# A hybrid encoder layer: four x tiles normed before the first projection block, the first pair's attention bias on ScalarE's queue, and three score blocks set into a projection

## The chip, the cores and the metric

The kernel runs on one core of a Trainium2 chip. The metric is the device time of one execution in microseconds (us); of several executions the median is given. PE is TensorE (its matmuls; PEld its weight loads), DVE is VectorE, ACT is ScalarE, POOL is GpSimd, SP is SyncE, which does no arithmetic here and issues most transfers (DMAs).

## The reference

One layer over a sequence of 1024 rows with 1024 columns, in float32:

```
h   = rmsnorm(x, norm_mix_w) * (1 + scale_m(c)) + shift_m(c)
P   = h @ w_in                     # z, xbc, dt, q, k, v in one projection
y_s = mamba2_ssd(z, xbc, dt)       # 8 heads of 64
q.. = chunks of 64 rows; each attends to its own chunk and 8 before it, 8 heads of 64
s   = q @ k^T / 8 + rel_bias[head][clipped distance]   # invalid keys: minimum
y_a = softmax(s) @ v
x   = x + gate_m(c) * (concat[y_s, y_a] @ w_out)
h   = rmsnorm(x) * (1 + scale_f(c)) + shift_f(c)
g,v = split(causal_dwconv3(h @ w_up));  x = x + gate_f(c) * ((silu(g) * v) @ w_down)
out = rmsnorm(x)
```

scale, shift and gate are columns of `c @ w_ada`.

## The kernel before

The float32 products are made of rounded parts: a matrix is split into a high part (`hH`, `wsh`, `wh`) and the rest (`hL`, `wsl`, `wl`), and a product is three matmuls (`mm3`: high by high, low by high, high by low). Sequence rows come in 8 tiles of 128 (`xts[0..7]`; the traces call them `qk`, since they share that store), and the 1024 columns in 8 slices `kt`. A half `hh` is four row tiles.

**The opening.** For each `kt` the kernel loads two 512 KB pieces of `w_ada` (`adat`), multiplies each with the row of c and sums it on DVE (`mod_col`, one reduction of 128x1024 each), which gives the column's scale and shift (`amix`, `bmix`); loads the piece of `w_first` (q and k of the first pair and v; `raws`), rounds it on ACT (`wsh`) and takes the rest on DVE (`wsl`). The x tiles are normed row by row: `x_square` (ACT, or DVE as a reduction), `x_rstd` (add EPS on DVE, power -0.5 on POOL), `x_scale` (ACT or DVE). `h_block(hh, kt)` transposes four normed tiles on PE (`tp`), and ACT makes `hH` and `hf` of them with `amix` and `bmix`, DVE `hL`. Then `first_qk` (accumulators `acc`) and `first_v` (`vps`) multiply. For `kt` = 0 this is done in two halves of two tiles: tiles 2 and 3 are loaded after the first weights and normed after the first half's `hH`. `kt` 6 and 7 of `acc` come as a tail, after the v products. Tiles 4 to 7 are loaded and normed amid the later `kt`; their loads wait for a DVE copy (`XL`), their ACT and DVE work for a block (`XS`, `XM`). Before the first block PE runs 8 and then 12 matmuls on the identity (`warm_up`, `WARM`).

**The attention.** A pair `p` is two heads; its 8 blocks `i` of 128 queries attend to up to 640 keys. `attn_scores` does for each block and head: two matmul groups into a `s` tile (`scores`; two such tiles in all, one for each head), a DVE reduction that adds the bias and takes the row's extreme (L529), exp on ACT (L532), a reciprocal on DVE (L534), the scaling on POOL (L535). `attn_pv` transposes the scaled rows on PE (`tp`, L561 and L564), splits them (`pt`, ACT and DVE) and multiplies with v (`pv`). Blocks 0 to 2 of pair 0 take the bias from a small tile that is loaded early (`rows`); from block 3 on it is the tile `bias`, 128x640, one for each head, loaded on SP's queue, and two corners of it are set to -1e30 by POOL (the masks, L591 and L592). `gemm_part(2, 0)` is the projection of a later pair's q: 8 `kt` of three matmuls for each half, in one accumulator `acc`. Between the first half's matmuls and the second's it needs that accumulator copied out by DVE (`ev`, L236).

**What sets the order.** A scheduler places each engine's instructions in one row by its own model of times. `tc.issue_after(x)` holds an instruction behind another one in that order; `InOrder` (`V`, `A`, `T` while `.on`) chains the instructions of an engine in the order of the code, and those have line L61 in the profile, whatever they do. SP's queue issues in its row's order and stops at the first transfer whose buffer or source is not free.

Of the kernel before, what the change touches and what calls it, by code (L numbers as in the profile page):

```python
# [10 lines left out]
F32 = mybir.dt.float32  # L11
# [5 lines left out]
P = 128  # L17
# [12 lines left out]
PRST = 4  # L30
GP, GPL = {0: (0,1), 2: (2,)}, ()
# [3 lines left out]
WARM = (8, 12)  # L35
# [32 lines left out]
def tile_block(ctx: ExitStack, tc: tile.TileContext, x, ccol, pk, w_ada, w_first, w_ft, w_z,  # L68
# [58 lines left out]
    G.memset(mhalf, -0.5)  # L127

# [74 lines left out]
    def mod_shift(dst, sh, kt, n=1):  # L203
        V.tensor_tensor(dst[:, kt:kt + n], modc[:, sh + kt:sh + kt + n],
                        pkt[:, B_ADA + sh + kt:B_ADA + sh + kt + n], ALU.add)
# [55 lines left out]
    def scores(p, i):  # L261
        d = qk[p]
        j0 = max(0, i - 4)
        n = (i - j0 + 1) * P
        off = (j0 - (i - 4)) * P
        parts = [(0, n)] if n <= 512 else [(0, 320), (320, 320)]
        st = [s_tile(), s_tile()]
        for h in range(2):
            for pi, (a, w) in enumerate(parts):
                for ti, kn in enumerate(("kh", "kl")):  # L270
                    T.matmul(st[h][:, 512 * pi:512 * pi + w], d["q"][h][:, i * P:(i + 1) * P],
                             d[kn][h][:, j0 * P + a:j0 * P + a + w], start=ti == 0, stop=ti == 1)
        return st, n, off, parts


# [36 lines left out]
    def x_square(st, eng):  # L312
        ms = stat()
        junk = s0.tile([P, D], F32, tag="junk", name="junk")
        if eng is A:
            i = norm_to(xts[st], junk, ms)
        else:
            i = V.tensor_tensor_reduce(out=junk, in0=xts[st], in1=xts[st], scale=1.0 / D, scalar=0.0,
                                       op0=ALU.mult, op1=ALU.add, accum_out=ms)
        return ms  # L320

    def x_rstd(ms):
        r = stat()
        V.tensor_scalar(ms, ms, EPS, None, op0=ALU.add)
        G.tensor_tensor(r, ms, mhalf[:, 0:1], ALU.pow)
        return r
# [15 lines left out]
    for st in range(2):  # L342
        x_load(st)
# [21 lines left out]
    r0 = x_rstd(ms0)  # L365
    r1 = x_rstd(x_square(1, V))
    x_scale(0, r0, A)
    x_scale(1, r1, A)
# [27 lines left out]
    for hh in range(2):  # L396
# [13 lines left out]
        for kt in range(KT):  # L410
            if hh == 0:
                mod_col(SC_M + kt, wu.tile([P, 1024], F32, tag="wh", name="adat"))
                mod_col(SH_M + kt, adw[:, kt % 2, :])
                V.scalar_tensor_tensor(amix[:, kt:kt + 1], modc[:, SC_M + kt:SC_M + kt + 1],
                                       pkt[:, NMIX + kt:NMIX + kt + 1], am1[:, kt:kt + 1],
                                       op0=ALU.mult, op1=ALU.add)
                mod_shift(bmix, SH_M, kt)
                t = raw_tile(768)
                nc.sync.dma_start(t, w_first[kt])
                split(wsh[:, kt, :], ws_lo(kt), t, A, V)  # L420
                if kt == 0:
                    for st in (2, 3):
                        x_load(st)
                    for b in range(2):
                        if b:
                            with tc.issue_after(hb[0].ins):
                                r = [x_rstd(x_square(st, A)) for st in (2, 3)]
                            x_scale(2, r[0], V)
                            x_scale(3, r[1], V)
                        hb = h_block(0, 0, (2 * b, 2 * b + 1))  # L430
                        T.on = False
                        for n in range(4):
                            first_qk(accs[n], n, 0, (0,), slice(2 * b, 2 * b + 2))
                        first_v(vps, 0, (0,), (b,))
                        V.on = A.on = T.on = False
                    continue
                for st in range(4, NT):
                    if XL[st - 4] == kt:
                        V.tensor_copy(xts[st][:, 0:1], amix[:, kt:kt + 1])
                        x_load(st)  # L440
            if hh == 0 or kt > 1:
                hb = i, last_lo = h_block(hh, kt)
            if hh == 0:
# [71 lines left out]
    def attn_scores(p, i, bt):  # L515
        st, n, off, parts = s00 if p + i == 0 else scores(p, i)
        res = []
        for h in range(2):
# [16 lines left out]
            G.tensor_scalar(pv_, pv_, rr, 1.0, op0=ALU.mult, op1=ALU.mult)  # L535
# [46 lines left out]
    last_v, early = [], {}  # L582
    mtq, todo = [], [m + kt for m in (G_M, SC_F, SH_F, G_F) for kt in range(KT)]

    def attention(p, extra=()):
        extra = dict(extra)
        bt = []
        for h in range(2):
            t = bp.tile([P, 640], F32, tag="bias", name="bias")
            nc.sync.dma_start(t, bias[2 * p + h])  # L590
            G.memset(t[0:64, 576:640], -1e30)  # L591
# [15 lines left out]
    def gemm_ft(wh, wl, outs):  # L607
        for hh in range(2):
            for kt in range(KT):
                w = slice(kt * P, (kt + 1) * P)  # L610
                mm3(c4(outs[hh]), wh[:, w], wl[:, w], *ht(hh, kt), kt == 0, kt == KT - 1)

    def gemm_part(p, which):
# [8 lines left out]
        gemm_ft(wh, wl, outs)  # L622
# [1065 lines left out]
```

## Time and profile before

| | |
|---|---|
| median of 3 runs | 1205.41 us (1205.05 to 1207.55) |
| profiled execution: its own time | 1205.95 us |
| profiled execution: span | 1204.2 us |
| granted TensorE clock, mean | 0.986 of full |
| busy: PE, DVE, ACT, POOL | 1168.7, 909.1, 587.5, 156.5 us |
| DMA | 160.24 MB, mean 133 GB/s |

The span runs from the first to the last instruction; 1.75 us of the execution's own time lie outside it. Of the span PE is idle for about 35.5 us in all. A row of a timeline gives the start in us, the duration, the engine, the line, the operation, output <- inputs by the program's names, and in brackets the idle time before it and what ended it. Matmul records overlap: a row's duration has the matmul's latency in it, and the distance between two starts is the pace. A row of the windows gives, behind the stretch, its length and the busy time (and instructions) of PE, PEld, DVE, ACT and POOL, the granted clock, the busy share of the DMA engines and what they moved in GB/s.

### The profile page before, as it was taken

Reading aid. Unit: us, or ns where it says so; the run is one execution under the profiler, and the core shown is the slowest. Engines: PE = TensorE matmul, PEld = TensorE weight load, DVE = VectorE, ACT = ScalarE, POOL = GpSimd, SP = SyncE. Lnnn points to the kernel's source line nnn. Section 1 sums busy time; section 2 is a strip of 40 time slices with the busy share of each in tenths; the row PEclk is TensorE's granted clock in tenths of the full one; section 3 lists DMA queues with packets and bytes.
Section 4 is the critical chain, followed back from the end, with each engine's and each line's share of the span. In section 5 each row is a group of like instructions: output and inputs, shape, how many; then the busy total and the mean of one; then the engine's idle time right before and its main releaser. Section 6 shows DMA issues by size and latency. Waiting matters only on the chain.

```text
span 1204.2 us, 15722 instructions
## 1 busy us (share of the span) xinstructions
PE 1168.7 (97%) x5823; PEld 980.8 (81%) x5823; DVE 909.1 (75%) x1364; ACT 587.5 (49%) x968; POOL 156.5 (13%) x177
## 2 busy tenths in 40 slices
PE   8998999899999899999999999999999999999996
PEld 6777888788889888888788888888888888888885
DVE  7645565775596888658999988898889879766986
ACT  6534564674243757577534443344333445433454
POOL 1002342530000344200000000000000000000522
PEclk8998999999999989999999999999999999999998
DMA  9635434301486322140232323322233378733443
GB/s 357 244 84 136 110 108 116 108 1 36 153 273 222 124 66 93 53 164 30 79 139 98 102 92 105 131 81 98 94 121 114 110 250 299 258 114 122 158 132 149
DMA packets 61293, 160.24 MB, mean 133 GB/s; under 512 B 6608, under 2 KB 7072, under 8 KB 59808
## 3 DMA queue, kind: packets, MB, share of 16 engines
q1 hardware_dynamic: 54160, 134.85, 34.2%
q10 hardware_dynamic: 7056, 24.38, 5.1%
q8 instruction: 46, 0.75, 0.3%
q14 instruction: 31, 0.25, 0.1%
HBM read 121.15 MB, written 28.61 MB: 124 GB/s over the span
## 4 chain that ended last, share of the span: by engine, by line
PE 85%; DVE 8%; issue 3%; DMA 2%; ACT 1%; SPq 1%; POOL 0%; POOLq 0%; DVEq 0%; ACTq 0%
PE wops L827 6%; PE dn L81 5%; PE dn L79 5%; PE dn L80 5%; PE uY L79 5%; PE uY L81 5%; PE uY L80 5%; PE uX L81 3%; PE uX L79 3%; PE uZ L80 3%; PE uZ L79 3%; PE uX L80 3%; PE uZ L81 3%; PE s L79 3%; PE s L80 3%
## 5 line engine op out<-in xcount | busy, mean ns | idle before, releaser
L80 PE MATMUL dn<-w 128*128 128x512 f32 x296 | 108.1, 392 | 0.0
L79 PE MATMUL dn<-w 128*128 128x512 f32 x296 | 108.1, 391 | 0.0
L81 PE MATMUL dn<-w 128*128 128x512 f32 x296 | 100.2, 391 | 0.2 <-DVE w L89 0.2
L79 PE MATMUL uY<-tH,w 128*128 128x512 f32 x248 | 97.2, 392 | 0.0
L80 PE MATMUL uY<-tL,w 128*128 128x512 f32 x248 | 97.0, 391 | 0.0
L81 PE MATMUL uY<-tH,w 128*128 128x512 f32 x248 | 96.9, 391 | 0.0
L1549 POOL TENSOR_TENSOR ya<-ya,xs 128x512 f32<-128x512 f32 x4 | 17.2, 4330 | 557.6 <-ACT xs L1545 557.6
L88 ACT ACTIVATE w<-ya 128x1024 fp32r<-128x1024 f32 (+1 forms) x41 | 39.2, 957 | 87.3 <-PE uY L81 84.2
L827 PE MATMUL wops<-hH,yhl 128*128 128x512 f32 x224 | 73.4, 401 | 0.0
L81 PEld LDWEIGHTS dn<-w 128*128 128x128 f32 x296 | 55.4, 188 | 13.2 <-DVE w L89 1.1
L79 PEld LDWEIGHTS dn<-w 128*128 128x128 f32 x296 | 55.5, 188 | 12.3
L80 PEld LDWEIGHTS dn<-w 128*128 128x128 f32 x296 | 55.5, 188 | 12.2
L535 POOL TENSOR_SCALAR p<-p,st 128x640 f32<-128x640 f32 (+4 forms) x64 | 49.3, 776 | 108.3 <-DVE st L534 95.2
L529 DVE CUSTOM_DVE_ANT_0 p<-s,bias 128x640 f32<-128x640 f32 (+4 forms) x58 | 38.3, 676 | 29.2 <-PE tp L561 10.3
L88 ACT ACTIVATE w<-xs 128x1024 fp32r<-128x1024 f32 (+1 forms) x41 | 39.1, 954 | 37.3 <-PE uY L81 33.3
L89 DVE TENSOR_TENSOR pt<-tp,pt 128x512 fp32r<-128x512 f32 (+2 forms) x72 | 42.0, 596 | 18.1 <-ACT pt L88 17.7
L81 PEld LDWEIGHTS uY<-tH,w 128*128 128x128 f32 x248 | 46.6, 188 | 10.5
L79 PEld LDWEIGHTS uY<-tH,w 128*128 128x128 f32 x248 | 46.5, 188 | 10.3
L80 PEld LDWEIGHTS uY<-tL,w 128*128 128x128 f32 x248 | 46.6, 188 | 10.2
L79 PE MATMUL s<-hH,wh 128*128 128x512 f32 x128 | 50.6, 395 | 1.2 <-DVE ct L636 1.0
L88 ACT ACTIVATE pt<-tp 128x512 fp32r<-128x512 f32 (+2 forms) x72 | 36.8, 525 | 29.9 <-PE tp L561 15.4
L1223 DVE SCALAR_TENSOR_TENSOR a<-cv,pkt,a 128x1023 f32<-128x1023 f32 (+1 forms) x40 | 51.0, 1277 | 0.1
(492 smaller groups left out, 3422.4 us busy)
## 6 DMA issues: line engine op xcount, KB each, us to landing
wos<-in_w_ada_dram SPq DMA_DIRECT2D x24, 512.0 KB, 4.6
gz<-a ACTq DMA_DIRECT2D x10, 1024.0 KB, 5.0
ya<-in_w_up_dram SPq DMA_DIRECT2D x11, 768.0 KB, 4.1
xs<-in_w_up_dram SPq DMA_DIRECT2D x11, 768.0 KB, 4.3
adat<-in_w_ada_dram SPq DMA_DIRECT2D x16, 512.0 KB, 7.6
raws<-in_w_ft_dram SPq DMA_DIRECT2D x14, 512.0 KB, 3.8
qk<-qk SPq DMA_DIRECT2D x56, 128.0 KB, 2.3
gy<-a ACTq DMA_DIRECT2D x10, 512.0 KB, 2.6
```

Source lines behind the costliest of these rows:

```text
L79: T.matmul(ps, lh, rh, start=start, stop=False, skip_group_check=more)
L80: T.matmul(ps, lh, rl, start=False, stop=False, skip_group_check=more)
L81: T.matmul(ps, ll, rh, start=False, stop=stop, skip_group_check=more)
L88: i = A.activation(hi, src, AF.Copy) if ehi is A else ehi.tensor_copy(hi, src)
L89: return i, elo.tensor_tensor(lo, src, f32(hi), ALU.subtract)
L529: V.tensor_tensor_reduce(out=dst, in0=src, in1=bsl, scale=-1.0, scalar=3e38, op0=ALU.add, op1=ALU.min, accum_out=nm)
L535: G.tensor_scalar(pv_, pv_, rr, 1.0, op0=ALU.mult, op1=ALU.mult)
L827: i = op(*a, **k)
L1223: V.scalar_tensor_tensor(a[:, j:S], c[:, 0:S - j], w[2 - j], a[:, j:S], op0=ALU.mult, op1=ALU.add)
L1549: G.tensor_tensor(src, src, fnr[:, halves[1]], ALU.mult)
```

## The change

Seven edits, in two places of the program.

In the opening: the x tiles 0 to 3 are loaded first of all, ahead of the first `w_ada` pieces, and normed before the first block (tiles 0 and 2 squared on ACT, 1 and 3 on DVE; tile 1 scaled on DVE, the others on ACT); EPS enters in the squaring on DVE, or by a 128x1 activation on ACT, in place of a DVE instruction; `kt` 0 is one block of four tiles, as the other `kt` are; its `wsh` is rounded on DVE; `mod_col` of a `kt` is held behind the `bmix` of the one before; the second run of identity matmuls is 26 long, not 12.

In the attention: the bias of pair 0 is issued on ScalarE's queue; its masks come in POOL's row behind the scaling of block 1 (of the later pairs: head 0's behind a scaling four from the last, head 1's behind the last); and the matmuls of `kt` 1, 3 and 5 of `gemm_part(2, 0)`, first half, are held behind the scores of blocks 1, 2 and 3.

```diff
+GPIN = {1: (0, 1), 3: (0, 2), 5: (0, 3)}
-WARM = (8, 12)
+WARM = (8, 26)
+    G.memset(mhalf[:, 7:8], EPS)
...
                     last = T.matmul(st[h][:, 512 * pi:512 * pi + w], d["q"][h][:, i * P:(i + 1) * P],
+        slast[p, i] = last.ins
...
         if eng is A:
-            i = norm_to(xts[st], junk, ms)
+            norm_to(xts[st], junk, ms)
+            A.activation(ms, ms, AF.Identity, bias=mhalf[:, 7:8])
...
-        V.tensor_scalar(ms, ms, EPS, None, op0=ALU.add)
...
-    for st in range(2):
+    for st in range(4):
         x_load(st)
...
-    x_scale(0, r0, A)
-    x_scale(1, r1, A)
+    x_scale(0, x_rstd(ms0), A)
+    x_scale(1, x_rstd(x_square(1, V)), V)
+    x_scale(2, x_rstd(x_square(2, A)), A)
+    x_scale(3, x_rstd(x_square(3, V)), A)
...
-                mod_col(SC_M + kt, wu.tile([P, 1024], F32, tag="wh", name="adat"))
-                mod_col(SH_M + kt, adw[:, kt % 2, :])
+                at = last_lo.ins if kt == 1 else bm.ins if kt else None
+                mod_col(SC_M + kt, wu.tile([P, 1024], F32, tag="wh", name="adat"), at)
+                mod_col(SH_M + kt, adw[:, kt % 2, :], at)
...
-                if kt == 0:
-                    for st in (2, 3):
-                        x_load(st)
-                    for b in range(2):
...
+                with tc.issue_after(bm.ins) if not kt else ExitStack():
+                    (A.activation(wsh[:, kt, :], t, AF.Copy) if kt else V.tensor_copy(wsh[:, kt, :], t))
+                with tc.issue_after(bm.ins):
+                    V.tensor_tensor(ws_lo(kt), t, f32(wsh[:, kt, :]), ALU.subtract)
...
-            nc.sync.dma_start(t, bias[2 * p + h])
-            G.memset(t[0:64, 576:640], -1e30)
-            G.memset(t[64:128, 0:64], -1e30)
+            (nc.sync if p else nc.scalar).dma_start(t, bias[2 * p + h])
             bt.append(t)
+        def masks():
+            for h, t in enumerate(bt):
+                with tc.issue_after(last_g[-1 if h or not p else -5]):
+                    G.memset(t[0:64, 576:640], -1e30)
+                    G.memset(t[64:128, 0:64], -1e30)
+        if p:
+            masks()
         for u in range(4):
             pa = attn_scores(p, 2 * u, bt)
             pb = attn_scores(p, 2 * u + 1, bt)
+            if p + u == 0:
+                masks()
...
-                mm3(c4(outs[hh]), wh[:, w], wl[:, w], *ht(hh, kt), kt == 0, kt == KT - 1)
+                with tc.issue_after(slast[pins[kt]]) if not hh and kt in pins else ExitStack():
+                    mm3(c4(outs[hh]), wh[:, w], wl[:, w], *ht(hh, kt), kt == 0, kt == KT - 1)
```

PE's row where the first block begins, before: `tp` with L282 are the transposes of x, `acc` is q and k, `vps` is v, and 128x256 is a half block.

```order
L61 MATMUL vps<-wsh,hL_85 128x256
L61 MATMUL vps<-wsh,hH_83 128x256
L61 MATMUL vps<-wsl,hH_83 128x256
L61 MATMUL vps<-wsh,hL_85 128x256
L282 MATMUL tp_243<-ident,qk 128x128
L282 MATMUL tp_278<-ident,qk 128x128 x3
L282 MATMUL tp_243<-ident,qk 128x128
L282 MATMUL tp_278<-ident,qk 128x128
L79 MATMUL acc_190<-hH_83,wsh 128x256
```

The same place now, right behind the identity matmuls (`warm`):

```order
L62 MATMUL warm<-ident 128x128 x26
L62 MATMUL tp_231<-ident,qk 128x128 x2
L286 MATMUL tp_274<-ident,qk 128x128 x2
L62 MATMUL tp_231<-ident,qk 128x128
L286 MATMUL tp_274<-ident,qk 128x128
L62 MATMUL tp_231<-ident,qk 128x128
L286 MATMUL tp_274<-ident,qk 128x128
L80 MATMUL acc_215<-hH_84,wsh 128x512
```

The second half's transposes stood behind a finished first half; now all eight transposes (tiles 0 to 3, for `kt` 0 and 1) stand ahead of one block with 512 columns.

PE's row at the start of the attention, before: `acc` is the projection of a later pair, `s` the scores of a block (256 columns are block 1, 384 block 2, 512 block 3, 320 one part of block 4), `tp` and `pv` belong to blocks that have been scaled.

```order
L81 MATMUL acc<-hH_83,wl 128x512
L271 MATMUL s<-qk 128x256 x4
L79 MATMUL acc<-hH_83,wh 128x512
L80 MATMUL acc<-hL_85,wh 128x512
L81 MATMUL acc<-hH_83,wl 128x512
L561 MATMUL tp<-ident,p 128x128 x2
L271 MATMUL s<-qk 128x384 x4
L564 MATMUL tp<-ident,p 128x128 x2
L271 MATMUL s<-qk 128x512 x4
L564 MATMUL tp<-ident,p 128x128 x2
L572 MATMUL pv<-pt,v 128x256
L271 MATMUL s<-qk 128x320 x4
```

The same place now, from the last matmuls of `kt` 4 on:

```order
L82 MATMUL acc<-hH_84,wl 128x512
L555 MATMUL tp<-ident,p 128x128 x2
L273 MATMUL s<-qk 128x512 x4
L80 MATMUL acc<-hH_84,wh 128x512
L81 MATMUL acc<-hL_86,wh 128x512
...
L558 MATMUL tp<-ident,p 128x128 x4
L273 MATMUL s<-qk 128x320 x8
```

Blocks 1 and 2 stand further up, each behind one or two more `kt`; block 3 is ahead of `kt` 5, 6 and 7 (nine matmuls, of which two are shown), and the transposes that need the scaled blocks 1 come after these, where before they stood between blocks 2, 3 and 4.

POOL's row there, before: `bias` are the masks, `p` the scaling of blocks 0 (128), 1 (256), 2 (384).

```order
L535 TENSOR_SCALAR p<-p,st_72 128x128 x2
L591 MEMSET bias 64x64
L592 MEMSET bias 64x64
L535 TENSOR_SCALAR p<-p,st_72 128x256
L591 MEMSET bias 64x64
L592 MEMSET bias 64x64
L535 TENSOR_SCALAR p<-p,st_72 128x256
```

And now:

```order
L529 TENSOR_SCALAR p<-p,st_72 128x128 x2
L529 TENSOR_SCALAR p<-p,st_72 128x256 x2
L590 MEMSET bias 64x64
L591 MEMSET bias 64x64
L590 MEMSET bias 64x64
L591 MEMSET bias 64x64
L529 TENSOR_SCALAR p<-p,st_72 128x384 x2
```

Each scaling of block 1 stood behind one head's masks, which need that head's bias; now both stand ahead of all masks.

More of the change, by code (lines that the diff above doesn't have):

```diff
@@ L315, in x_square @@
         if eng is A:
[L316 to L319 removed]
+            norm_to(xts[st], junk, ms)
+            A.activation(ms, ms, AF.Identity, bias=mhalf[:, 7:8])
+        else:
+            V.tensor_tensor_reduce(out=junk, in0=xts[st], in1=xts[st], scale=1.0 / D, scalar=EPS,
+                                   op0=ALU.mult, op1=ALU.add, accum_out=ms)
         return ms
@@ L442, in tile_block @@
                 hb = i, last_lo = h_block(hh, kt)
+            if hh == 0 and kt == 0:
+                V.on = A.on = T.on = False
             if hh == 0:
```

30 lines of the change are left out of this document (8 added, 22 removed).

## The prediction

> **What bounds the kernel now.** I read the page first: its busy times, and the chain that ended last.
>
> ```profile
> span 1204.2 us, 15722 instructions
> PE 1168.7 (97%) x5823; PEld 980.8 (81%) x5823; DVE 909.1 (75%) x1364; ACT 587.5 (49%) x968; POOL 156.5 (13%) x177
> PE 85%; DVE 8%; issue 3%; DMA 2%; ACT 1%; SPq 1%; POOL 0%; POOLq 0%; DVEq 0%; ACTq 0%
> ```
>
> PE is idle for 1204.2 - 1168.7 = 35.5 us, which is the most that better order alone could save at this clock. So I looked for where it idles, and where it is busy at a low clock, with busy time by stretches of 20 and of 4 us.
>
> ```profile
> 0.00:20.00 20.00, 14.60 (x70) 11.74 (x70) 12.19 (x29) 11.28 (x18) 5.28 (x14) 0.91 0.90 342
> 20.00:40.00 20.00, 19.34 (x111) 17.40 (x112) 19.14 (x43) 10.14 (x15) 0.00 (x0) 0.91 1.00 380
> 100.00:120.00 20.00, 16.45 (x84) 14.17 (x82) 11.19 (x41) 10.09 (x29) 7.22 (x17) 0.83 0.46 126
> ...
> 20.00:24.00 4.00, 3.77 (x19) 3.77 (x20) 4.00 (x10) 3.05 (x6) 0.00 (x0) 0.57 1.03 408
> 104.00:108.00 4.00, 1.64 (x10) 1.14 (x8) 2.03 (x11) 1.80 (x6) 0.72 (x3) 1.00 0.87 225
> 112.00:116.00 4.00, 4.00 (x18) 3.80 (x17) 2.76 (x9) 3.01 (x8) 1.22 (x3) 0.50 0.00 0
> 116.00:120.00 4.00, 3.99 (x29) 3.54 (x27) 3.81 (x13) 3.30 (x10) 2.41 (x4) 0.98 0.01 4
> ```
>
> Two stretches stand out, and the change touches just these: the opening, where PE idles and the clock is low until about 24, while DVE is busy for 19.14 of 20 us and the DMA share is 1.00; and 100 to 120, where PE is idle 20 - 16.45 = 3.55 us and then runs at half clock for about seven (a mean of 0.83 over 20 us is 6.8 at half). Behind about 230 us the order of every engine is as before, and PE is the bound there, so a gain or a loss in these stretches passes to the end.
>
> **The opening.** PE's, DVE's and POOL's timelines give the pace:
>
> ```profile
> 8.74 1.84 PE L61 MATMUL warm<-ident 128*128 128x128 f32 x15
> 12.85 0.74 PE L79 MATMUL acc<-hH,wsh 128*128 128x256 f32 x4 [0.86 <-ACT hH L61]
> 20.23 0.96 PE L79 MATMUL acc<-hH,wsh 128*128 128x256 f32 x4 [0.55 <-ACT hH L289]
> 24.70 1.10 PE L79 MATMUL acc<-hH,wsh 128*128 128x512 f32 x4
> 29.09 0.39 PE L79 MATMUL acc<-hH,wsh 128*128 128x512 f32 x1
> 47.99 0.38 PE L282 MATMUL tp<-ident,qk 128*128 128x128 f32 x2
> 50.64 0.39 PE L61 MATMUL vps<-wsh,hL 128*128 128x256 f32 x1 [0.40 <-DVE hL L293]
> 52.57 0.39 PE L61 MATMUL acc<-hH,wsh 128*128 128x512 f32 x1
> ...
> 7.38 1.23 DVE L61 CUSTOM_DVE_ANT_0 junk<-qk 128x1024 f32<-128x1024 f32 x1 [0.47 <-DMA qk<-in_x_dram]
> 8.79 1.23 DVE L61 CUSTOM_DVE_ANT_0 adat<-adat,rows 128x1024 f32<-128x1024 f32 x1
> 15.92 0.75 DVE L332 TENSOR_SCALAR qk<-qk,st 128x1024 f32<-128x1024 f32 x1
> 35.01 0.96 DVE L89 TENSOR_TENSOR wsl<-raws,wsh 128x768 fp32r<-128x768 f32 x1
> 36.43 1.23 DVE L138 CUSTOM_DVE_ANT_0 adat<-adat,rows 128x1024 f32<-128x1024 f32 x1 [0.47 <-DMA adat<-in_w_ada_dram]
> 49.89 0.69 DVE L293 TENSOR_TENSOR hL<-hf,hH 128x512 fp32r<-128x512 f32 x1 [2.18 <-ACT hf L290]
> ...
> 8.88 1.54 POOL L325 TENSOR_TENSOR st<-st,mhalf 128x1 f32<-128x1 f32 x1 [1.26 <-DVE st L61]
> ...
> 10.46 1.15 ACT L61 ACTIVATE qk<-qk,st 128x1024 f32<-128x1024 f32 x1 [0.89 <-POOL st L325]
> ```
>
> Before, the block of `kt` 0 is done in two halves, from 12.85 and from 20.23, and ends at 24.70; a whole block takes 29.09 - 24.70 = 4.39.
>
> Start of the one block now. Tile 1 is there at 7.38. Tiles 2 and 3 follow it on the queue; 0.524 MB at 342 GB/s is 1.5 us, less if it runs at the 408 of a full stretch: about 9.9 for tile 3. Its reduction on DVE (1.23) ends at 11.2, then two powers on POOL, one after the other, 1.54 each (13.9 at the latest), the scaling on ACT 1.15, the transposes and `hH` about 1.2: **16.3**. So the products begin 3.5 us later than the first half did and 3.9 earlier than the second. The 14 more identity matmuls (15 took 1.84 in PE's row, so about 1.7) lie in this wait; without that cover they would cost 1.7.
>
> DVE is the price. The two `w_ada` pieces of `kt` 0 come behind two more x tiles, so the first `mod_col` starts near 11.3, not 8.79. Against these 2.5 us stand two row scalings (0.75 each; one of them moves in front of the weights, one to ACT) and the eight EPS instructions on one column that go; and DVE now waits once, for `hf` of `kt` 0 (about 17.6), which holds all later `mod_col`. The rounding of `wsh` (taken between 0.55, a guess from the half-sized `hL`, and 0.96, the `wsl` row) falls into that wait. I get `wsl` of `kt` 5 ended at 37.0 to 37.6 instead of 35.97: DVE 1.0 to 1.6 late. PE can stand this: in the new order each `kt` begins with the `hH` products and wants `hL` 1.9 us later. With 4.4 for each `kt` it would be through `kt` 5 near 44.5, before 47.99; if all of `kt` 0 runs at half clock, near 47.
>
> So the end of the opening is set by the last column's data. Before, from the end of `wsl` of `kt` 5 (35.97) to the end of the last `hL` (49.89 + 0.69 = 50.58) DVE took 14.6 us. Its work in it, put end to end at the rows' durations less the tenth by which neighbours overlap, is four `mod_col` of 1.15, two `wsl` of 0.9, four `hL` of 0.6 and about 0.6 of single columns: 9.4. The other 5.2 were waits, nearly all for ACT, which waited for PE's transposes. From 37.3 on that is 46.7 with no wait and 51.9 with all of them. The transposes come up to 3.5 us sooner (47.99 to 44.5), so I take 3.5 off the 5.2: 46.7 + 1.7 = 48.4. The hL products of `kt` 7 then start at 48.4 where they started at 50.64: **-2.2 us**. Ends: -3.6 (PE's own limit, the 3.5 and a little idle) and +1.3 (all waits kept).
>
> **The attention.** The rows, PE first, then POOL, SP, DVE, and one of the chain in order of time:
>
> ```profile
> 98.61 0.39 PE L79 MATMUL acc<-hH,wh 128*128 128x512 f32 x1
> 103.39 0.63 PE L271 MATMUL s<-qk 128*128 128x256 f32 x4
> 104.69 0.95 PE L271 MATMUL s<-qk 128*128 128x384 f32 x4
> 108.10 0.44 PE L564 MATMUL tp<-ident,p 128*128 128x128 f32 x2 [2.46 <-POOL p L535]
> 108.29 1.19 PE L271 MATMUL s<-qk 128*128 128x512 f32 x4
> 111.27 1.27 PE L271 MATMUL s<-qk 128*128 128x320 f32 x4
> 123.86 0.50 PE L79 MATMUL acc<-hH,wh 128*128 128x512 f32 x1 [0.16 <-DVE ev L236]
> ...
> 107.13 0.14 POOL L591 MEMSET bias<- 64x64 f32 x1 [6.02 <-DMA bias<-in_bias_dram]
> 109.60 0.14 POOL L591 MEMSET bias<- 64x64 f32 x1 [1.55 <-DMA bias<-in_bias_dram]
> ...
> 95.67 7.64 SPq L230 DMA_DIRECT2D qk<-qk  x11
> 104.59 1.08 SPq L590 DMA_DIRECT2D bias<-in_bias_dram  x2
> ...
> 115.69 0.82 DVE L529 CUSTOM_DVE_ANT_0 p<-s,bias 128x640 f32<-128x640 f32 x1
> 123.13 0.68 DVE L236 SCALAR_TENSOR_TENSOR ev<-acc,qk 128x512 fp32r<-128x512 f32 x1
> ...
> 105.22 4.58 DMA bias<-in_bias_dram
> ```
>
> SP issues eleven moves in 7.64 us before the biases; the masks wait for these, and the scaling of block 1 stands behind the masks; PE wants that block scaled for its next transposes, and idles. Meanwhile the projection's matmuls, which need nothing of this, are used up by 103.39.
>
> Now the bias is issued behind the last v copy on ACT, about 99.4 (0.8 after the last v product, 98.61), and lands 4.6 later by the chain's row, 104.0; ACT waits there for the second of the eleven moves only, which has landed by then, and the exps of block 0 queue some 1.1 us behind the two issues. The scaling of block 1 no longer waits for it. The masks then end near 105.
>
> PE from 98.61 to block 4: 24 projection matmuls at (103.39 - 98.61) / 21 = 0.228 are 5.46; blocks 1 to 3 by their rows 0.63 + 0.95 + 1.19, each less the 0.16 by which a matmul's row (0.39) exceeds its pace, 2.29; six transposes 0.6: 8.35 in all, so block 4 at **107.0**, where it was at 111.27: -4.3. From block 4 to DVE's fifth block (115.69) it was 4.42, and I keep that, since DVE now has the reciprocals of blocks 1 to 3, which wait for exps, in front of these reductions: 111.4. From there to `ev` (123.13) it was 7.44; the new order has one 640-wide reduction less in it (0.8), so `ev` at 118.0 and the projection's second half at 118.7 where it was at 123.86: -5.2. That chain has little slack left, so I take **-5.0**. Ends: -6.0 (DVE at full pace, and none of the low clock) and -2.0 (bias landing two to three late, reductions of block 3 waiting for masks). For the later pairs the masks only move behind scalings, at 0.3 us on an idle POOL: nothing.
>
> Here the Trainium skill speaks against the change. DMA: Bandwidth & Descriptors, Issuing engines are not separate DMA queues, says that a transfer runs on the same 16 engines whichever engine issues it, so that another issuer saves only the time of issuing, usually small. By that the move of the bias would bring about 1 us (SP's row of 1.08 for two issues). The row above has the time at stake otherwise: 7.64 us of moves in the queue before it.
>
> **Sum.** -2.2 - 5.0 = -7.2: the profiled execution's 1205.95 becomes 1198.8. It lies 0.54 above the median of 1205.41, so the median becomes **1198.2**.
>
> **The rivals.**
>
> *Only the attention gains.* DVE's lateness and the full DMA engines (1.00, 380 GB/s) keep the last column at 50.6, opening 0: 1200.4. For it: `mod_col` of `kt` 6 already waited for its piece (0.47 at 36.43). Against: the 2.18 wait at 49.89 is not of DMA. Chance 0.2.
>
> *The bias lands no sooner.* The eleven moves and the bias share the engines; if the bias lands at 109 as before, the reductions of block 3 wait for masks until about 110, and only the projection's better place is left, -0.7 instead of -5.0: -2.9 in all, 1202.5. It decides from a landing later than 107. For it: DMA share 0.87 at 104 to 108. Against: 225 GB/s there, far from the 408 of a full stretch. This is the case that the skill's sentence above describes. Chance 0.1.
>
> *The low clock lasts.* After the idle 2.46 us the clock was at half for about seven although PE was busy 4.00 of 4. The change makes a new wait of some 2.7 us between the identity matmuls and 16.3. If half clock then holds through `kt` 0 to 2, these end at 16.3 + 3 x 8.8 = 42.7 and `kt` 5 at 55.9; the `vps` of `kt` 6 and 7 and their transposes, 3.2, bring the tail to 59.1 where it began at 52.57: +6.5. The like in the attention, where about 10 us of PE's work stand between block 4 and the second half, gives the 5.0 back: 1211.9. The opening's loss outweighs the attention's gain and 2.4 us more only if the attention's is gone too; that decides. Against: at 20:24 PE was busy 3.77 of 4 at 0.57, and full right after. The Trainium skill (TensorE: Matmul & The Clock Gate, Part 1: The HAM clock gate) has full clock return after about 3.4 us of sustained work, by which this rival fails in both places; the rows, with seven, are less kind. Chance 0.06.
>
> *It does not do what it says.* The pins could leave the rows as they were: 1205.4. The new rows of PE and POOL show that they do not; what is left is that both gains are eaten within 2.4 us. Chance 0.06.
>
> The forecast itself has the rest, 0.58.
>
> **How the numbers follow.** 0.2% (2.4 us) is about what a measurement of this kernel tells from no change. Best of both stretches: -3.6 - 6.0 = -9.6, 1195.8. The upper end reaches over the first two rivals: 1202.5 and 0.5 for the spread of runs, 1203.0. The low end gets the same 0.5: 1195.3. Faster by over 0.2%: forecast, first rival and most of the second, 0.86; within it 0.07; slower 0.07.
>
> **What would show it.** In the new profile: one `kt` 0 block of 128x512 from about 16.3; PE's wait for `hL` of `kt` 7 ending near 48.4, the `acc` tail from 50.3; no idle of over 1 us in 98 to 107, the granted clock 1.00 at 108 to 116; block 4 (128x320) near 107, the bias issued by ACT near 99.4, the second half of the projection near 118.7. I am wrong if `mod_col` of `kt` 1 to 5 runs more than 2 us late, if ACT stands before its first exp, or if the low clock is still there in those stretches. Behind 230 us every row should be shifted by the same amount.

## The result, and the profile after

| | before | changed |
|---|---|---|
| median, first comparison | 1205.74 us (1204.59 to 1207.55, 6 runs) | 1199.15 us (1196.78 to 1200.24, 6 runs) |
| median, second comparison | 1205.45 us (12 runs) | 1198.41 us (1197.31 to 1201.64, 6 runs) |
| profiled execution: time, span | 1205.95, 1204.2 us | 1199.13, 1197.4 us |

The ratio is 0.9943 with a 95% interval of 0.993 to 0.9955, and 0.9947 (0.9931 to 0.9963) in the second comparison: 6.9 and 6.4 us faster. The forecast was 1198.2, 7.2 us faster.

The page of the changed kernel, first the busy times, then the chain that ended last:

```profile
span 1197.4 us, 15744 instructions
PE 1166.5 (97%) x5839; PEld 979.5 (82%) x5839; DVE 909.2 (76%) x1357; ACT 588.5 (49%) x970; POOL 157.4 (13%) x178
PE 82%; DVE 10%; issue 3%; ACT 2%; DMA 1%; POOL 1%; POOLq 0%; DVEq 0%; ACTq 0%; SPq 0%
```

PE is idle for 30.9 us, not 35.5, and busy for 2.2 us less with the same products. It has 16 records more: 28 for the longer identity run, and 12 fewer because the products of `kt` 0 now come in one block. The first difference is waiting, the second clock. The windows of the changed kernel show both:

```profile
0.00:20.00 20.00, 17.39 (x104) 14.94 (x105) 12.52 (x27) 11.54 (x18) 4.71 (x15) 1.00 0.91 343
20.00:40.00 20.00, 19.20 (x118) 16.84 (x117) 19.84 (x44) 11.53 (x17) 1.45 (x1) 1.00 1.00 374
100.00:120.00 20.00, 19.58 (x119) 16.85 (x118) 14.21 (x45) 14.09 (x35) 10.78 (x22) 1.00 0.51 146
```

The granted clock is 1.00 where it was 0.91, 0.91 and 0.83, and PE is idle for 0.42 us of 100 to 120 instead of 3.55. In the opening, PE's timeline and then DVE's:

```profile
7.75 5.86 PE L62 MATMUL warm<-ident 128*128 128x128 f32 x51
15.76 1.19 PE L80 MATMUL acc<-hH,wsh 128*128 128x512 f32 x4 [0.76 <-DVE wsl L62]
47.23 0.39 PE L62 MATMUL vps<-wsh,hH 128*128 128x256 f32 x1 [1.51 <-ACT hH L293]
48.63 0.39 PE L62 MATMUL vps<-wsh,hL 128*128 128x256 f32 x1 [0.40 <-DVE hL L297]
50.56 0.39 PE L62 MATMUL acc<-hH,wsh 128*128 128x512 f32 x1
...
35.48 0.95 DVE L428 TENSOR_TENSOR wsl<-raws,wsh 128x768 fp32r<-128x768 f32 x1
42.13 0.96 DVE L428 TENSOR_TENSOR wsl<-raws,wsh 128x768 fp32r<-128x768 f32 x1 [2.15 <-ACT wsh L426]
47.88 0.69 DVE L297 TENSOR_TENSOR hL<-hf,hH 128x512 fp32r<-128x512 f32 x1 [0.69 <-ACT hf L294]
```

The one block begins at 15.76 (16.3 forecast), the last column's `hL` products at 48.63 (48.4), the tail at 50.56 (50.3; before 52.57). In the attention, PE, then ACT and SP, POOL and DVE:

```profile
95.78 0.39 PE L80 MATMUL acc<-hH,wh 128*128 128x512 f32 x1
104.02 1.42 PE L273 MATMUL s<-qk 128*128 128x320 f32 x8
114.37 0.50 PE L80 MATMUL acc<-hH,wh 128*128 128x512 f32 x1 [0.22 <-DVE ev L238]
134.65 0.50 PE L80 MATMUL acc<-hH,wh 128*128 128x512 f32 x1 [0.82 <-DVE qk L247]
...
95.99 1.04 ACTq L584 DMA_DIRECT2D bias<-in_bias_dram  x2
92.81 10.78 SPq L232 DMA_DIRECT2D qk<-qk  x11
...
100.13 0.94 POOL L529 TENSOR_SCALAR p<-p,st 128x256 f32<-128x256 f32 x2 [1.16 <-DMA qk<-qk]
102.11 0.14 POOL L590 MEMSET bias<- 64x64 f32 x1 [0.77 <-DMA bias<-in_bias_dram]
105.08 0.81 DVE L523 CUSTOM_DVE_ANT_0 p<-s,bias 128x640 f32<-128x640 f32 x1
113.64 0.67 DVE L238 SCALAR_TENSOR_TENSOR ev<-acc,qk 128x512 fp32r<-128x512 f32 x1
```

The first projection matmul (95.78) is 2.83 us earlier than before. Block 4 follows it after 8.24 us (12.66 before, 8.35 forecast) and the second half after 18.59 (25.25 before). So 6.66 us are gained in this stretch where the forecast had 5.0.

### The profile page after: what moved, and what is told of

It reads as the page before. It is cut to its first block, busy times and chain, and to the rows that moved or that the text cites. A ratio compares the mean times of both kernels' runs of the same rounds, so it can differ in the third digit from the quotient of the medians.

```text
span 1197.4 us, 15744 instructions
## 1 busy us (share of the span) xinstructions
PE 1166.5 (97%) x5839; PEld 979.5 (82%) x5839; DVE 909.2 (76%) x1357; ACT 588.5 (49%) x970; POOL 157.4 (13%) x178
## 4 chain that ended last, share of the span: by engine, by line
PE 82%; DVE 10%; issue 3%; ACT 2%; DMA 1%; POOL 1%; POOLq 0%; DVEq 0%; ACTq 0%; SPq 0%
PE wops L831 6%; PE dn L82 5%; PE dn L80 5%; PE dn L81 5%; PE uY L80 5%; PE uY L82 5%; PE uY L81 5%; PE uX L82 3%; PE uX L80 3%; PE uZ L81 3%; PE uZ L80 3%; PE uX L81 3%; PE uZ L82 3%; PE s L80 2%; PE s L81 2%
## 5 line engine op out<-in xcount | busy, mean ns | idle before, releaser
L526 ACT ACTIVATE p<-p,st 128x640 f32<-128x640 f32 (+4 forms) x64 | 44.0, 690 | 13.6 <-DVE st L523 13.0
```

Source lines behind the costliest of these rows:

```text
L526: A.activation(pv_, pv_, AF.Exp, scale=-1.0, bias=nm, accum_out=rs)
```

## The experiments

All kernels are compared with the kernel before on the same chip. "Tail" is the start of the `acc` tail in the profile. "Attention" is what the kernel gains on the one before from the projection's first matmul (98.61 there) to a matmul of a later projection (214.12 there), ahead of which the orders have done the same work; its rows for the two kernels:

```profile
214.12 0.40 PE L79 MATMUL acc<-hH,wh 128*128 128x512 f32 x1
```

```profile
205.11 0.39 PE L80 MATMUL acc<-hH,wh 128*128 128x512 f32 x1
```

So the changed kernel gains 214.12 - 205.11 = 9.01 to there, 2.83 of it in the opening, 6.18 in the attention. Two kernels have done a little less by then: bias_sp and pins_only have four score matmuls (0.16 us each) fewer ahead of that matmul and one of `pv` (0.12) more, so their gain is too high by about 0.5 us, an estimate.

| kernel | ratio (95% interval) | median us | tail | attention |
|---|---|---|---|---|
| before | 1 | 1205.4 to 1206.6 | 52.57 | 0 |
| changed | 0.9943 (0.993 to 0.9955) | 1199.15 | 50.56 | 6.18 |
| changed, again | 0.9947 (0.9931 to 0.9963) | 1198.41 | 52.68 | 6.27 |
| open_only | 0.9977 (0.9967 to 0.9987) | 1202.99 | 50.60 | 2.47 |
| attn_only | 0.995 (0.9936 to 0.9964) | 1200.18 | 52.53 | 6.34 |
| warm12 | 0.9964 (0.9951 to 0.9977) | 1201.81 | 54.66 | 6.33 |
| warm26_before | 1.0016 (1.0005 to 1.0027) | 1207.22 | 58.32 | 1.38 |
| bias_sp | 0.9943 (0.993 to 0.9955) | 1199.26 | 51.08 | 6.12 |
| no_gpin | 0.9955 (0.9942 to 0.9967) | 1199.45 | 51.06 | 5.02 |
| masks_old | 0.9963 (0.9949 to 0.9976) | 1201.11 | 52.58 | 5.08 |
| pins_only | 0.9947 (0.9931 to 0.9962) | 1199.58 | 52.48 | 5.73 |
| masks_only | 0.9965 (0.9953 to 0.9978) | 1201.71 | 51.09 | 2.90 |
| fill_z | 0.9966 (0.9953 to 0.9979) | 1200.72 | 51.46 | 6.29 |
| fill_z18 | 0.9955 (0.9939 to 0.9971) | 1200.52 | 50.88 | 6.28 |

Tail and attention are of one profile each, and hold what the clock did in it: in the stretch of "attention" the kernel before ran 6.83 us at half clock, warm26_before and pins_only 3.41, all others nothing.

**The halves of the change.** open_only has the edits of the opening and leaves the attention's order as it was; attn_only has the edits of the attention and the opening as it was.

> The opening's edits alone; the attention's edits (bias queue, place of the masks, pins of the projection) are as before. By the prediction's steps: the acc tail begins 2.0 to 2.2 us earlier than before (52.57), so near 50.5, and the attention's start runs as before, shifted: 1203.0 to 1203.6 in the median. If what the changed kernel gives back behind 230 us (9.5 us ahead at its second half of the projection, 6.8 at its end) is a floor, something that does not move with PE, then this kernel alone, only 2.8 ahead, should keep all of it: 1202.9 or less. If it is a matter of where the clock and the waits happen to fall, then this kernel may give back up to 1.5 as well: 1203 to 1204.5.

> The attention's edits alone; the opening is as before. From the first projection matmul to the second half of the projection it should take 18.6 us as in the changed kernel, not 25.25: -6.6 at that place. By the prediction's term for the attention (-5.0): 1200.7. If all of -6.6 stayed: 1199.1. If a floor eats what is beyond 6.8, as in the changed kernel, none of 6.6 is eaten: 1199.1, and the opening would be worth nothing on top. If the two parts add: about 1201.5.

Measured: 2.8 and 6.0 us by the ratios. Their sum is 8.8, the whole is 6.4 to 6.9; with intervals of 1.2 to 1.9 us on each side the halves may add or overlap by some 2 us, and the runs don't tell which. The rival "only the attention gains" falls: the opening alone is faster, with its interval clear of 1.

open_only also shows what part of the old stretch was clock. Its windows, and PE's wait for block 1's scaling:

```profile
103.00:107.00 4.00, 1.37 (x6) 0.85 (x6) 1.30 (x7) 1.78 (x5) 1.43 (x6) 1.00 0.89 264
111.00:115.00 4.00, 3.99 (x29) 3.52 (x28) 3.95 (x13) 3.91 (x10) 2.62 (x4) 1.00 0.01 4
105.45 0.44 PE L558 MATMUL tp<-ident,p 128*128 128x128 f32 x2 [2.61 <-POOL p L529]
```

The wait is there, yet the clock stays at 1.00, where the kernel before had 0.50 at 112 to 116. With the attention's order unchanged it "gains" 2.47 us there, and warm26_before, also with the old order and half the low clock, 1.38: so much of the first pair's 6.18 is a low clock that the old order does not always get, and 3.7 to 4.8 are left for the new order, 3.7 with the clock at 1.00 on both sides.

**The longer run of identity matmuls.** warm12 sets it back; warm26_before is the kernel before with the long run.

```diff
-WARM = (8, 26)
+WARM = (8, 12)      # warm12, in the changed kernel; warm26_before the reverse, in the kernel before
```

> The changed kernel with 12 identity matmuls in the second run in place of 26. By the prediction these only fill a wait, and leaving them out changes nothing: within 0.5 of the changed kernel. Rival: they hold the clock. Then PE waits about 1.7 us more ahead of the first block, the granted clock falls to half for some 7 to 10 us from about 13, kt 0 takes 8 instead of 4.5, and the acc tail begins 0.5 to 2 later than 50.56: 1 to 2 us slower in all.

> The kernel before with 26 identity matmuls in place of 12, nothing else. If the opening's gain is the clock that they hold, and the one block of kt 0 only goes with it: the clock stays at full from 13 on, the acc tail begins 1.5 to 2 earlier than 52.57, and the kernel is 1.5 to 2 faster than before. If they only fill a wait, or if the wait between the halves (1.67 and 0.55 us at 19 to 20) drops the clock anyway: 0 to 0.5 faster, or slower by up to 1, since the first half's transposes now stand behind the longer run.

warm12, PE's timeline at the first block and two windows:

```profile
13.93 0.33 PE L62 MATMUL tp<-ident,qk 128*128 128x128 f32 x1 [3.21 <-ACT qk L62]
16.27 1.22 PE L80 MATMUL acc<-hH,wsh 128*128 128x512 f32 x2 [0.76 <-DVE wsl L62]
16.00:20.00 4.00, 3.73 (x13) 3.34 (x14) 3.33 (x8) 1.63 (x3) 0.29 (x2) 0.50 1.04 401
20.00:24.00 4.00, 4.00 (x18) 3.34 (x17) 4.00 (x11) 2.18 (x3) 0.00 (x0) 0.71 0.98 351
```

Without the 14 matmuls PE waits 3.21 us, the block begins at about the same time, and the clock is at 0.50 and 0.71 behind it; the tail comes at 54.66, 2 to 4 us later than in the changed kernel, which is 2.5 us faster. So they do not only fill a wait: they keep the clock. They are no guarantee: bias_sp has all 26, waits of 0.71 and 0.76 us in place of the 3.21, and half clock for 3.41 us from 16.79 on all the same:

```profile
16.00:20.00 4.00, 3.73 (x14) 3.31 (x15) 3.33 (x8) 1.62 (x3) 0.29 (x2) 0.60 1.06 405
```

There it cost nothing: the last `hL` starts 32.14 us behind the block, as in the changed kernel (32.13), where warm12, with 6.83 us at half, needs 34.96.

In the kernel before the same 14 cost 1.9 us (0.6 to 3.3). Its profile is the slowest of the twelve executions (1209.9 us), so the tail of 58.32 shows more than that. The first half's products begin at 14.52 instead of 12.85 there, the wait between the halves stays, and the clock still falls. The long run paid only together with the one block.

**Bias, masks and pins.** bias_sp puts the bias back on SP's queue, masks_old the masks back to their place in the code, no_gpin takes the pins of `kt` 1, 3 and 5 away; pins_only and masks_only keep just the one of the three. open_only has none.

```diff
-            (nc.sync if p else nc.scalar).dma_start(t, bias[2 * p + h])
+            nc.sync.dma_start(t, bias[2 * p + h])       # bias_sp, pins_only, masks_only
-GPIN = {1: (0, 1), 3: (0, 2), 5: (0, 3)}
+GPIN = {}                                               # no_gpin, masks_only
-        if p:
-            masks()
+        masks()                                         # masks_old, pins_only: pair 0's not held behind a scaling
```

> The changed kernel with pair 0's bias back on SP's queue; the masks and the pins stay. By the prediction: the bias is issued behind the eleven moves, near 100.6, lands 105 to 106.5 instead of about 101 and 102, the reductions of block 3 wait for the masks, block 4's scores come 3 to 4 us later than 104.0, and the kernel is 3 to 4 us slower than the changed one: about 1202.5. By the rule that another issuer saves only the time of issuing (1.08 us for two): about 1 us slower, 1200.2.

> The changed kernel with pair 0's masks ahead of the scaling again, as far as the planner puts them; bias on ScalarE's queue and pins stay. In the changed kernel the second head's mask waited for its bias until 102.11. With the masks ahead of the scalings, the scaling of block 0 should wait until about 101 (98.24 there) and that of block 1 until about 102.5, PE's first transposes wait 0.5 to 1 at 100.5: 0.5 to 1 slower than the changed kernel. If POOL's row does not matter once the bias is early: no difference.

> The changed kernel without the three pins: the projection's matmuls run ahead of block 1's scores as before, bias queue and masks stay changed. By the prediction's working the pins put the scores of block 1 four us sooner, so that exp and scaling lie behind matmuls; without them PE idles again, though less than 2.46 + 1.09 since the scaling no longer waits for the masks: block 4's scores 1.5 to 2.5 later than 104.0, the kernel 1.5 to 2.5 slower than the changed one. Rival: the queue and the masks are the whole of it, and the pins bring nothing: within 0.5 of the changed kernel.

> The new opening and the new place of block 1 to 3's scores, but the bias on SyncE's queue and the masks at their old place in the code. If queue and place of the masks count only locally: the stretch from the first projection matmul to the second half 20 to 22.5 us (changed kernel 18.59, before 25.25), and at the end within 1.5 us of the changed kernel, about 1199 to 1200.5. Prediction's sum (bias 3.5 us earlier is what the gain of the attention rests on): 3 us slower than the changed kernel, about 1202.

> The new opening and the masks behind block 1's scaling, but the bias on SyncE's queue and the scores at their old place. If the masks now make block 2's scaling wait for a bias that lands near 104.5 to 106: stretch from the first projection matmul to the second half 20 to 23 us, and the kernel 1.0 to 3.0 us slower than the changed one (1200 to 1202.5). Rival (the clock alone made the 2.5 us of the stretch, the edits of the attention little): as the new opening alone, 1202.5 to 1203.5.

bias_sp, SP's and POOL's timelines:

```profile
92.85 7.62 SPq L232 DMA_DIRECT2D qk<-qk  x11
100.51 0.58 SPq L584 DMA_DIRECT2D bias<-in_bias_dram  x1
104.57 0.15 POOL L590 MEMSET bias<- 64x64 f32 x1 [2.38 <-DMA bias<-in_bias_dram]
106.17 0.15 POOL L590 MEMSET bias<- 64x64 f32 x1 [1.25 <-DMA bias<-in_bias_dram]
```

The queue does what was said of it: on SP the bias stands behind the eleven moves (the second head's is issued at 101.77, after one move more), and the second mask comes at 106.17 instead of 102.11, or, counted from the projection's first matmul, at 9.87 instead of 6.33. The end does not show it: 0.9943 both times, and 6.12 (5.6 for equal work) against 6.18 us in the attention. With intervals of 1.5 us on each side that excludes the 3 to 4 us expected, but cannot tell the 1 us of the rule from nothing. In this order the scheduler has moved work of PE ahead of the projection's second half (118.68, 4.3 us later than in the changed kernel), and has that much less behind it. The distance from the projection's first matmul to its second half, by which the expectations reckon, is therefore no measure across orders: 22.38 in bias_sp, 19.79 in masks_old, 20.25 in no_gpin, 22.80 in pins_only, 22.44 in masks_only, against 18.59. pins_only is 1.2 us slower than the changed kernel on its chip, which is inside their intervals, and not 3; masks_only 3.3, a little over what was expected.

In the profiles the pins and the early bias stand in for each other. Gain in the attention, with the ratio of the whole time:

| | bias on ACT | bias on SP |
|---|---|---|
| pins, masks new | 6.18, 6.27 (0.9943, 0.9947) | 6.12 (0.9943) |
| pins, masks old | 5.08 (0.9963) | 5.73 (0.9947) |
| no pins, masks new | 5.02 (0.9955) | 2.90 (0.9965) |
| no pins, masks old | not run | 2.47 (0.9977) |

Without pins the early bias is worth 5.02 - 2.90 = 2.1 us, with them 0.1 (0.6 for equal work). The pins are worth 3.2 to 3.3 with the bias on SP (2.7 for equal work) and 1.2 with it on ACT. With neither, hardly anything is gained over what full clock gave the old order: 2.90 against 2.47. masks_only's second mask waits for its bias until 108.50, and PE 1.36 us for POOL at 109.57. With the pins PE has projection matmuls left while POOL waits: in pins_only the second mask comes at 107.91, and no wait of PE is over 0.93, though half clock came all the same, from 110.82 to 114.23. The whole times mostly cannot tell these kernels apart: masks_old, at 0.9963, is even out of order. The difference of pins_only to open_only alone is clear (0.9931 to 0.9962 against 0.9967 to 0.9987).

The place of the masks counts where the bias is early: in masks_old POOL has the first mask ahead of the scaling of block 0 and starts that 5.15 us behind the projection's first matmul instead of 2.45; the attention gains 1.1 us less. With the bias on SP the scheduler sets the masks behind the scaling of block 2 in bias_sp and in pins_only alike, so those two differ by 0.4 only.

**The wait ahead of the SSD's output products.** In both kernels PE waits 4.79 us for `zs` (the rows of z and dt, which DVE finishes) behind the last z projection, before at 421.73, now at 413.56, and the clock is low behind it. fill_z and fill_z18 put 38 and 19 identity matmuls there; nobody reads their result.

```diff
+        if (ch, st) == (0, NT - 1):
+            fill = tp_tile()
+            for _ in range(19):        # fill_z: 38
+                T.matmul(fill[:, 0:P], ident, ident, start=True, stop=True)
```

> The changed kernel with 38 identity matmuls more, placed behind the last z projection, where PE waits 4.79 us for DVE at 409 to 413.6 (they compute nothing that is used). If what was given back between 413 and 447 is the clock that falls in such waits: the chunk's first 16 matmuls take 1.9 instead of 3.7, the granted clock is 1.00 from 412 to 444, PE's wait for th at 427.8 begins and ends 1.7 earlier, and the kernel is 1.7 to 2.8 faster than the changed one: 1196.5 to 1197.5. If DVE's work sets the pace there and the clock does not matter: no difference.

> The changed kernel with 19 identity matmuls behind the last z projection (38 passes of about 0.23 us by the first filling experiment, 4.3 us, inside the wait of 4.79 us ahead of the output projection). Their result is read by nobody. Clock theory: the granted clock stays 1.00 from 412 us, the 16 output-projection matmuls take 1.9 us instead of 3.7, and the kernel is 1.0 to 2.8 us faster than the changed one of the same batch. Rival (VectorE's chain through zs and th sets the pace there, the clock only fills its waits): no difference over 0.5 us, with a longer wait behind the output projection.

38 were too many: they ran from 409.85 to 418.11, 4.6 us past the old start. That is 0.22 us a matmul, of two records each (the expectation of fill_z18 has this as 0.23 a pass; its 4.3 us are right for 19 matmuls). 19 fit, and the clock stayed. fill_z18, PE's timeline and three windows:

```profile
414.12 2.00 PE L835 MATMUL ydp<-xdt,th 128*128 128x64 f32 x16 [0.53 <-DVE zs L784]
428.66 3.64 PE L835 MATMUL ydp<-xdt,th 128*128 128x64 f32 x16 [3.76 <-DVE th L867]
412.00:420.00 8.00, 7.47 (x52) 6.75 (x51) 5.08 (x7) 6.04 (x16) 7.97 (x7) 1.00 0.25 81
420.00:428.00 8.00, 3.84 (x19) 2.71 (x17) 7.90 (x10) 5.19 (x14) 4.88 (x5) 0.90 0.00 1
428.00:436.00 8.00, 7.34 (x26) 6.65 (x27) 4.37 (x8) 1.26 (x2) 0.09 (x1) 0.50 0.21 65
```

At `wops` (the products of the output projection), 3.3 us further on, it is 10.7 us ahead of the kernel before. Then PE waits 3.76 us for `th` (the decay factors of the next rows), with DVE busy 7.90 of 8 us, the clock falls there instead, for 10.24 us, and at the next long stage only 3.8 us of lead are left. This profile is the slowest of the six (1202.14); their median is 1200.52 against 1198.41 for the changed kernel on the same chip, and the intervals of the two overlap, so it is not faster. In this profile DVE sets the stage's pace, and a full clock only lets PE reach the next wait sooner, as the rival had it.

**The changed kernel again.**

> The changed kernel once more, nothing left out, beside the other three on one chip. If the whole change is worth what the first comparison gave (0.9943), about 1198.5 to 1200.0 us here. Theory A (the granted clock after the waits differs from execution to execution): the time that the first profile gave back between 414 and 447 us, 1.3 us, need not be given back in this profile; the shift against the kernel before stays between 6.5 and 9.5 us at the end. Rival: the give-back is a property of the order, and the same 1.3 us go at the same place.

after_again, four windows:

```profile
48.00:52.00 4.00, 3.44 (x15) 3.04 (x16) 1.39 (x2) 4.00 (x7) 0.51 (x1) 0.61 0.35 133
412.00:420.00 8.00, 6.97 (x27) 6.54 (x28) 4.16 (x7) 4.89 (x14) 6.60 (x7) 0.50 0.17 60
420.00:428.00 8.00, 7.21 (x36) 5.89 (x34) 7.90 (x11) 4.72 (x12) 4.12 (x4) 0.94 0.02 6
428.00:436.00 8.00, 7.66 (x42) 6.60 (x42) 7.40 (x12) 3.61 (x11) 2.09 (x2) 1.00 0.17 66
```

The same program, and the clock falls at other places: at 48 to 52, where the first profile had 1.00, and not at 428 to 436, where it had 0.79:

```profile
48.00:52.00 4.00, 3.60 (x24) 3.17 (x25) 2.02 (x3) 3.97 (x9) 0.55 (x1) 1.00 0.40 131
428.00:436.00 8.00, 8.00 (x40) 6.96 (x41) 6.18 (x10) 3.38 (x10) 2.05 (x2) 0.79 0.17 66
```

(these two are the first profile's). The lead at `wops` is 8.70 us and 8.63 at the end, so the 1.3 us that the first profile gave back there are not of the order. The others agree: the five more profiles that have a second spell of half clock near 430 (open_only, bias_sp, masks_old, pins_only, warm26_before) lose 1.2 to 1.6 us of lead there, and attn_only, no_gpin, warm12 and masks_only, which have none, at most 0.5. None of the versions tried is measurably faster than the changed kernel.

## Why the prediction was right, and where its steps were not

**The total** came out within 1 us (1199.15 and 1198.41 against 1198.2), inside the likeliest case. Both stretches gained, but not for the reasons given in every step, and that the total fits so closely is in part luck: the attention gave more than its -5.0 against a profile with a low clock and less (3.7) against one without, the opening gave somewhat less, and the first profile lost part of its lead again behind 120.

**The start of the one block**: 15.76 in the first profile, 15.28 to 16.50 over the kernels with the new opening and the long run, against 16.3. The sum of tile, reduction, two powers and scaling came out with two errors that cancel: the reduction of tile 3 started at 10.54, behind ACT's square of tile 2, and ended at 11.8, not 11.2, while the two powers took 2.4 us together, not 3.1. And `hH` (15.70) is no longer alone: DVE's row of two `mod_col`, `wsh` and `wsl`, which the sum leaves out, ends at 15.73.

**The 14 more identity matmuls** were mis-sized. The working took 15 records for 15 matmuls and got 1.7 us. But one 128x128 matmul on the identity is two records: the row above has 51 of the 52 records of 26 matmuls, in 5.86 us, where the kernel before had, for 12:

```profile
7.74 2.84 PE L61 MATMUL warm<-ident 128*128 128x128 f32 x24
112.57 0.82 DVE L529 CUSTOM_DVE_ANT_0 p<-s,bias 128x640 f32<-128x640 f32 x1 [0.20 <-PE s L271]
```

(the second row is used under the attention.) So 14 take 3.1, not 1.7, and they fill the whole wait that the *low clock* rival relied on ("some 2.7 us"). In the opening that rival did not come about because of them: in warm12, with the wait, half clock held from 15.5 to 22.3. Not through `kt` 2, though, as its price assumed: warm12's tail came 2.1 us behind the old one (54.66 against 52.57), not 6.5. The Trainium skill (TensorE: Matmul & The Clock Gate, Part 1: The HAM clock gate) has full clock back after about 3.4 us of sustained work; in warm12 it came 6.1 us after the block's first product (16.27).

**DVE in the opening.** `wsl` of `kt` 5 was to end 1.0 to 1.6 us late, at 37.0 to 37.6; it ended at 36.4, 0.5 late. The last `hL` was to end at 48.4 and ended at 48.57. One sign of being wrong was touched: the first `mod_col` of `kt` 1 starts 2.25 us late (17.02 against 14.77), but by `kt` 3 (24.34 in both) nothing is left of it. From the start of the block to the start of this `hL` it takes 32.12 to 32.14 us in eight of the ten profiles with the new opening and the long run, 32.45 and 32.51 in the two with the earliest blocks: the data begins with the block and then runs at its own pace, with DVE busy 19.84 of the 20 us from 20 to 40.

**The end of the opening.** Forecast -2.2, the first profile -2.0, but -2.2 was no fixed amount. PE waits 1.4 to 1.5 us for the last column's `hH` near 47.5 in nine profiles with the new opening; in four the clock stays at 1.00 and the tail begins 34.8 us behind the block's start, in five it falls to 0.61 to 0.70 and it takes 35.8 to 36.4. bias_sp, with a wait of 1.09, takes 34.8 too. Among the ten with the long run the tail begins between 50.56 and 52.68, its median at 51.1: -1.5.

**The attention.** Block 4 came 8.24 us after the projection's first matmul; the count of 24 matmuls, three score blocks and six transposes gave 8.35. No wait of over 1 us was left, and the clock was 1.00. From block 4 to `ev` it took 9.62, not 11.0 (118.0 - 107.0), which is most of the difference between -5.0 and the -6.66 at the second half. The step mis-sized is the reduction less, at 0.8: before, eight 640-wide reductions stand between 112.57 and `ev` (10.56 us, 1.32 each), now seven from 105.08 (8.56 us, 1.22 each). So one less is worth 1.3 with the waits between them, and the others ran somewhat faster; how much of that is the low clock before, the rows don't tell. The -5.0 was set against a profile with low clock, though: 1.4 to 2.5 us of it would not recur, as the old order showed in two other kernels.

**The bias on ACT's queue** is the step that fell. The working had it as what the gain rests on, and the rival "the bias lands no sooner" left 0.7 of 5.0 from a landing later than 107, 8.4 us behind the projection's first matmul. In pins_only it lands so (mask at 107.91, 10.0 us behind it), and 5.73 us are gained. The step overlooked that the pins alone feed PE through the wait; only without them does the landing decide. It also took the row of 1.08 us for the two issues of pair 0: there the first head's bias is issued at 103.35, right behind the moves, and the second issue of that row is the next pair's. The Trainium skill (DMA: Bandwidth & Descriptors, Issuing engines are not separate DMA queues) says that another issuer saves only the time of issuing; the whole kernel's time does not speak against it (0.9943 both), the landing does (the mask 3.5 us earlier from the projection's first matmul, and 2.1 us of PE's time where there are no pins).

**"Behind 230 us every row shifted by the same amount"** was wrong. In the first profile the lead is 9.49 us at the second half, 8.40 at 335, 8.17 at 414 and 6.80 from 450 on. Of the 1.1 us that went by 335, about half went by 205 to new short waits, such as the 0.82 for `qk` at 134.65, and half between 229 and 256 to the clock: 6.83 us at half there, where the kernel before had 3.41. The 1.3 us behind 414 were the clock too, as the second profile shows.

**Faster by over 0.2%** had 0.86; both comparisons are, with their whole intervals.

## What to carry to other kernels

Hold independent matmuls back until the dependent work has been fed: with them in the right place the queue of a late transfer made no difference here that could be measured, and two cures of one wait must not be counted twice. Price a PE wait at its length and, on top, at a spell of half clock that it may or may not bring, and don't take one profile's gain for the change's where a clock row moved too. Filling a wait helps only if what follows is PE's own work; where another engine sets the stage's pace, the wait turns up again a few us on.

## What the hardware showed that was not expected

- Waits well under 3.4 us of PE brought a fall of the granted clock in some executions and none in others: 1.5 us near 47.5 in five of nine profiles, 2.46 us ahead of 108.10 in the kernel before, but not 2.61 ahead of 105.45 in open_only. The Trainium skill (TensorE: Matmul & The Clock Gate, Part 1: The HAM clock gate) puts the fall behind an idle window of about 3.4 us, and calls the window free-running; the second half fits the spread, the length does not.
- The spells of half clock lie on a grid. Within each of the 14 profiles they last 3.41, 6.83 or 10.24 us (all but the one at the kernel's end), and their starts are whole multiples of 3.413 us apart; where the grid lies differs from execution to execution. Cut along it, the kernel before has its wait of 2.46 us almost whole in one window, and open_only has its 2.61 us in two parts:

```profile
105.92:109.33 3.41, 1.23 (x6) 0.84 (x6) 0.87 (x5) 1.46 (x4) 0.77 (x3) 1.00 0.88 262
109.33:112.75 3.42, 2.33 (x11) 2.18 (x10) 2.39 (x8) 1.78 (x6) 2.15 (x7) 0.50 0.31 128
101.19:104.60 3.41, 1.65 (x10) 1.14 (x8) 2.05 (x11) 1.80 (x6) 0.12 (x1) 1.00 0.87 224
104.60:108.02 3.42, 2.22 (x13) 1.70 (x14) 1.53 (x4) 1.46 (x4) 2.18 (x9) 1.00 0.75 260
108.02:111.43 3.41, 3.25 (x23) 2.75 (x23) 3.41 (x14) 3.39 (x10) 2.06 (x4) 1.00 0.00 0
```

(two rows of the kernel before, three of open_only.) Between 10 and 1185 us of the 14 profiles the clock fell 49 times, always behind a window in which PE was busy for 2.38 us or less; every window at full clock with less than 1.59 us was followed by a fall, and of those between the two only some were. What decides between these the traces don't show.
- One 128x128 float32 matmul on the identity is two records in the trace, about 0.23 us together.
